# A second pair of tiles for the matrices of the triangular solve in a hybrid RWKV-7 diffusion backbone

## The chip, the cores and the metric

The kernel runs on one core of a Trainium2 chip. The metric is the device time of one execution in microseconds (us), the median of several runs. Engines are named as the profile names them: PE is the TensorE's matmul, PEld its weight load, DVE the VectorE, ACT the ScalarE, POOL the GpSimd, SP the SyncE, whose queue issues the DMA transfers here.

## What is computed

The reference is a backbone of two layers on 1024 latent tokens and 256 context tokens, 1024 wide. A layer makes a combined projection, gives its columns to four mixers (a bidirectional RWKV-7 scan, a pooling, a Fourier and a convolution mixer), concatenates, projects back, and ends in a SwiGLU feed-forward. The change concerns the RWKV-7 scan, a recurrence on a 64 x 64 state for each of four heads and two directions:

```python
def step(S, inp):
    w_t, kk_t, a_t, k_t, v_t = inp[:5]
    sa = jnp.einsum('bhvk,bhk->bhv', S, -kk_t)
    S = (S * w_t[:, :, None, :] + sa[..., None] * (kk_t * a_t)[:, :, None, :]
         + v_t[..., None] * k_t[:, :, None, :])
    y = jnp.einsum('bhvk,bhk->bhv', S, inp[5]) if with_out else None
    return S, y
...
for l in range(DEPTH):
    ...
    y_rwkv_x, y_rwkv_c = _rwkv_mixer(ux[..., :RWKV_COLS], uc[..., :RWKV_COLS], not last, ...)
    h = h + gt1 * _mix_and_project(ux, y_rwkv_x, *other)
    h = h + gt2 * _swiglu(_modulate(h, norm2_g[l], sh2, sc2), ffn_w_in[l], ffn_w_out[l])
```

## The kernel before

The scan is cut into stages: per layer two of the context (c0, c1) and eight of the latent tokens (x0 to x7), each 128 tokens of each direction and all heads. Inside a stage the recurrence is written in chunks of 64 tokens, for which a triangular system has to be solved. `rwkv2` (line 800) goes through the stages with generators that it steps in turn: for the stage at hand it runs `chain` (the states), and at the same time `front_b` and `finish` for its neighbours, `inner` of the stage two ahead and `prep` of the stage three ahead. Between the steps it takes pieces of other work as fill for PE, mostly `outp` (line 1648), the output projection of an earlier unit.

- `prep` (line 896) makes the decays and the scaled keys: tanh on ACT, an affine step on GpSimd (line 921), a running sum on the VectorE (line 926), exponentials on ACT, products on the VectorE and GpSimd (lines 942 to 971).
- `inner` (line 973) makes the matrices and solves. PE forms the Gram products in PSUM; the VectorE masks them (line 991, four instructions); SP stores the parts of interest to DRAM, eight transfers into `Ad` (line 995); SP loads them back in the shape that the solve wants, two transfers of 256 KB into `As` for a = 0 and 1 (line 1001). GpSimd then sets the diagonals to one (line 1029). The 4 x 4 diagonal blocks (lines 1031 to 1035) are solved on the VectorE for a = 0 and on GpSimd for a = 1. Eight steps follow on the VectorE (lines 1043 to 1052); the first four read `As` of a = 0, the last four that of a = 1. The result is stored to `Td` (line 1056) and read back in four transfers (line 1062).
- `front_b` (line 1069) and `chain` (line 1133) use the solved block.

Tiles come from `rg(R, name, depth)` (line 855): a ring of so many tiles under a name, handed out in turn. A ring of depth 1 gives the same tile each time, and the next stage's writer waits until the last reader of this stage is done. Every tile of a ring is a buffer of the pool `t2`, which has 73 of 128 x 512 floats; a ring holds its tiles to the end of the layer's scan. `outp` takes its readings of `ymix` (line 1657) and of the residual (line 1676) from the same pool; each reading of `ymix` is split in two (line 325, on GpSimd during the scan).

The order of instructions on an engine isn't the order of the code. A scheduler takes what is ready by its own estimate, by priorities; the solve (`ahead(SPRI)`) has a priority 1000 ahead of its place, and `pin` keeps some instructions in the order of the program. SP takes the DMA issues one after another, and an issue that waits holds up all behind it.

Of the kernel before, what the change touches and what calls it, by code (L numbers as in the profile page):

```python
# [92 lines left out]
class _Kernel:  # L93
# [879 lines left out]
    def inner(s, R, F):  # L973
# [21 lines left out]
                    nc.sync.dma_start(Ad[b, d, :, h].rearrange("u j i -> j u i"), W[r0:r0 + 32, :, 32 * b:32 * b + 32])  # L995
            yield

        As = [s.rg(R, f"As{a}", 1) for a in range(2)]
        Adf = Ad.rearrange("b d u h j i -> (b d u h) (j i)")
        for a in range(2):  # L1000
            nc.sync.dma_start(As[a], Adf[:, a * 512:(a + 1) * 512].unsqueeze(0).broadcast_to([4, 32, 512]))
# [890 lines left out]
```

## Time and profile before

| | |
|---|---|
| median of 3 runs | 3343.46 us (3340.38 to 3346.46) |
| the profiled execution | 3351.38 us, of which the span is 3349.6 us |
| mean granted clock of PE | 0.911 of full speed |
| PE, PEld busy | 90%, 72% of the span |
| DVE, ACT, POOL busy | 63%, 38%, 41% |
| DMA moved | 415.48 MB, 124 GB/s over the span |
| scan of the first layer | about 489 to 836 us of the span |
| scan of the second layer | about 2168 to 2549 us |

The profile is of one execution, and its times are counted from the start of its span. A chain is the work that ended last, followed back from the end; its shares are of the stretch asked for. A wait is idle time of an engine together with what ended it.

### The profile page before, as it was taken

What the parts mean: (1) busy time and instruction counts of PE and PEld (TensorE: products, weight loads), DVE (VectorE), ACT (ScalarE), POOL (GpSimd) and SP (SyncE); (2) the same over time, 40 slices, a digit from 0 to 9 for tenths busy, and PEclk for the clock granted to TensorE, in tenths of its full rate; (3) what the DMA queues carried; (4) which work ended last, traced back from release to release, by engine and by line L of the source; (5) the groups of instructions that cost most, each with busy time, mean ns of one, the idle gap of its engine ahead of it and who ended that gap; (6) DMA issues with size and microseconds to landing.
All of it is one profiled execution on the core that took longest, in us unless ns stands there. A gap on an engine that the chain in (4) does not pass through costs nothing.

```text
span 3349.6 us, 52386 instructions
## 1 busy us (share of the span) xinstructions
PE 3000.7 (90%) x18888; PEld 2410.5 (72%) x18888; DVE 2109.8 (63%) x3498; ACT 1257.5 (38%) x2575; POOL 1385.8 (41%) x1484
## 2 busy tenths in 40 slices
PE   6989997877889999999999978988877799999998
PEld 3657765766678888888888766756665588888787
DVE  6679666666374988644545598666665755554535
ACT  4446433443363222223212455333443433333212
POOL 2366224563168554435310064245550454545400
PEclk8989887787899999999999988987787799999999
DMA  7422344465455444337412212345553322224312
GB/s 265 165 92 97 102 117 136 124 174 156 144 190 164 149 132 151 125 98 233 139 35 78 87 53 90 117 134 139 156 159 88 128 92 79 82 89 164 123 39 78
DMA packets 375818, 415.48 MB, mean 124 GB/s; under 512 B 115587, under 2 KB 214916, under 8 KB 375558
## 3 DMA queue, kind: packets, MB, share of 16 engines
q1 hardware_dynamic: 375558, 412.13, 39.4%
q8 instruction: 149, 2.44, 0.3%
q14 instruction: 111, 0.91, 0.1%
HBM read 306.49 MB, written 100.27 MB: 121 GB/s over the span
## 4 chain that ended last, share of the span: by engine, by line
PE 55%; DVE 14%; DMA 9%; issue 3%; SPq 1%; ACT 1%; POOL 1%; DVEq 0%; POOLq 0%; ACTq 0%
PE pc L153 17%; PE ps L153 17%; PE pb L153 14%; PE pf L153 8%; DMA t<-Ad 3%; DVE c L532 2%; DMA Td<-t 1%; DVE t L1050 1%; DVE t L947 1%; DVE t L1043 1%; DVE f L325 1%; DVE t L956 1%; DVE t L1469 1%; DMA t<-ho 1%; DVE t L1493 1%
## 5 line engine op out<-in xcount | busy, mean ns | idle before, releaser
L153 PE MATMUL pc<-t,f 128*128 128x512 f32 (+1 forms) x3108 | 754.4, 392 | 41.3 <-ACT t L427 16.0
L153 PEld LDWEIGHTS pc<-t,f 128*128 128x128 f32 x3108 | 581.6, 195 | 182.9 <-ACT t L427 20.5
L153 PE MATMUL ps<-t,f 128*128 128x512 f32 (+1 forms) x2094 | 517.0, 393 | 18.4 <-ACT t L324 7.7
L153 PE MATMUL pb<-t,f 128*128 128x512 f32 (+1 forms) x2094 | 470.5, 370 | 8.4 <-ACT t L1468 4.9
L153 PEld LDWEIGHTS ps<-t,f 128*128 128x128 f32 x2094 | 390.8, 190 | 99.8 <-ACT t L324 8.2
L153 PEld LDWEIGHTS pb<-t,f 128*128 128x128 f32 x2094 | 370.4, 190 | 78.8 <-ACT t L1468 6.0
L1515 ACT CAST f<-c 128x512 fp32r<-128x512 f32 x316 | 196.0, 621 | 536.7 <-PE ps L153 132.0
L1517 POOL TENSOR_TENSOR f<-c,f 128x512 fp32r<-128x512 f32 x135 | 186.5, 1381 | 426.2 <-ACT f L1515 411.7
L153 PE MATMUL pf<-t,f 128*128 128x512 f32 (+2 forms) x1500 | 314.2, 364 | 14.2 <-DVE t L1044 4.0
L324 ACT CAST f<-m 128x512 fp32r<-128x512 f32 (+1 forms) x236 | 134.7, 576 | 436.3 <-PE pb L153 226.4
L153 PEld LDWEIGHTS pf<-t,f 128*128 128x128 f32 (+1 forms) x1500 | 249.5, 198 | 61.4 <-ACT f L324 4.4
L530 POOL TENSOR_TENSOR c<-c,cp 128x352 f32<-128x352 f32 (+2 forms) x168 | 183.3, 1092 | 145.9 <-ACT c L523 71.3
L1517 DVE TENSOR_TENSOR f<-c,f 128x512 fp32r<-128x512 f32 x181 | 158.6, 878 | 134.8 <-ACT f L1515 134.4
L153 PE MATMUL pf<-c,f 128*128 128x512 f32 (+1 forms) x704 | 200.5, 416 | 30.0 <-DVE t L1684 20.3
L325 POOL TENSOR_TENSOR t<-c,t 128x512 fp32r<-128x512 f32 (+1 forms) x110 | 135.1, 1266 | 173.8 <-PE ps L153 99.5
L153 PE MATMUL ps<-t,t 64*128 64x128 f32 (+2 forms) x1032 | 159.9, 341 | 38.9 <-DVE t L956 23.4
L532 DVE SCALAR_TENSOR_TENSOR c<-c,dv,c 128x352 f32<-128x352 f32 (+2 forms) x238 | 190.5, 829 | 2.0
L153 PEld LDWEIGHTS ps<-t,t 64*128 64x128 f32 (+1 forms) x1032 | 133.6, 231 | 60.4 <-issue 20.4
L153 PEld LDWEIGHTS pc<-t,t 128*64 128x64 f32 (+2 forms) x2484 | 124.6, 161 | 71.8 <-issue 28.6
L153 PE MATMUL pc<-t,t 128*64 128x64 f32 (+3 forms) x2484 | 156.2, 258 | 20.9 <-DMA t<-t 11.8
L153 PEld LDWEIGHTS pf<-c,f 128*128 128x128 f32 x704 | 131.5, 214 | 60.1 <-issue 19.1
L261 DVE SCALAR_TENSOR_TENSOR cp<-m,sc,cp 128x512 f32<-128x512 f32 x140 | 137.5, 1003 | 43.0 <-DMA m<-in_wmod 42.3
(256 smaller groups left out, 4731.3 us busy)
## 6 DMA issues: line engine op xcount, KB each, us to landing
c<-in_ffin SPq DMA_DIRECT2D x176, 256.0 KB
m<-in_wmod SPq DMA_DIRECT2D x116, 256.0 KB
t<-rw SPq DMA_DIRECT2D x232, 128.0 KB
hid<-t SPq DMA_DIRECT2D x88, 256.0 KB
c<-hid SPq DMA_DIRECT2D x88, 256.0 KB
m<-in_ffout SPq DMA_DIRECT2D x80, 256.0 KB
t<-in_wmod SPq DMA_DIRECT2D x76, 256.0 KB
m<-in_win SPq DMA_DIRECT2D x64, 256.0 KB
```

Source lines behind the costliest of these rows:

```text
L153: s.nc.tensor.matmul(o, l, r, start=start, stop=stop)
L261: nc.vector.scalar_tensor_tensor(acc[t], w, sc, acc[t], ALU.mult, ALU.add)
L324: r = s.nc.scalar.copy(hi, src)
L325: (eng or s.lo_eng).tensor_tensor(lo, src, hi.bitcast(F32), ALU.subtract)
L530: nc.gpsimd.tensor_tensor(g, g, t_, ALU.add)
L532: nc.vector.scalar_tensor_tensor(a, w[:, j:j + m], tap(j), a, ALU.mult, ALU.add)
L947: nc.vector.scalar_tensor_tensor(KRv[:, :, p, 0, 1:64], k2[:, :, p, 1:64], -2.0, P2[:, :, p, 0:63], ALU.mult, ALU.mult)
L956: nc.vector.tensor_tensor(BKv[rows, :, :, 1 - h, :], cv(kd)[rows], cv(iP)[rows], ALU.mult)
L1043: nc.vector.tensor_tensor(tv, at(x, o, [0, m], [1, 4], [32, 4]), at(T_, r0, [32, m], [0, 4], [1, 4]), ALU.mult)
L1050: nc.vector.tensor_tensor(tv, at(x, o + 4, [0, m], [1, n], [32, 4]), at(T_, r0, [32, m], [0, n], [1, 4]), ALU.mult)
L1515: nc.scalar.copy(hi, x)
L1517: (nc.gpsimd if s.nw % 7 in LOP else nc.vector).tensor_tensor(lo, x, hi.bitcast(F32), ALU.subtract)
```

## The change

`inner` takes its two `As` tiles from rings of depth 2 where they had depth 1. The stages then use two pairs of tiles in turn, and two more buffers of `t2` stay held through each scan. Nothing else in the code differs.

```diff
@@ -995,7 +995,7 @@
                     nc.sync.dma_start(Ad[b, d, :, h].rearrange("u j i -> j u i"), W[r0:r0 + 32, :, 32 * b:32 * b + 32])
             yield
 
-        As = [s.rg(R, f"As{a}", 1) for a in range(2)]
+        As = [s.rg(R, f"As{a}", 2) for a in range(2)]
         Adf = Ad.rearrange("b d u h j i -> (b d u h) (j i)")
         for a in range(2):
             nc.sync.dma_start(As[a], Adf[:, a * 512:(a + 1) * 512].unsqueeze(0).broadcast_to([4, 32, 512]))
```

Each engine has the same instructions as before; within the two scans their order is another. Three places follow. In the rows `Ad`, `Td`, `t`, `m`, `ho`, `hd` stand for the stored matrices, the solved block, tiles of `t2`, weights, the projection's output and the residual; line 302 loads weights, 876 slices of the scan's inputs.

SP in the second layer, around the loads of stage x2, before:

```order
L995 DMA Ad_21190<-t_3735_19993 32x4x32 x2
L995 DMA Ad_21190<-t_3737_19995 32x4x32 x2
L1685 DMA ho_17778<-t_3936_21254 128x512
L302 DMA m_3997_21795<-in_wout 128x512
L1001 DMA t_3662_19537<-Ad_21190 128x1x512
L302 DMA m_4000_21801<-in_wout 128x256
L1001 DMA t_3663_19538<-Ad_21190 128x1x512
L1056 DMA Td_21274<-t_3775_20164 4x256x32
L1676 DMA t_3966_21486<-hd_17788 128x512
L1676 DMA t_3987_21686<-hd_17789 128x512
L1676 DMA t_4003_21807<-hd_17790 128x512
L1062 DMA t_3759_20082<-Td_21274 32x8x32 x4
```

and after:

```order
L995 DMA Ad_21194<-t_3736_19994 32x4x32 x2
L995 DMA Ad_21194<-t_3738_19996 32x4x32 x2
L1056 DMA Td_21278<-t_3779_20168 4x256x32
L302 DMA m_3988_21684<-in_wout 128x256
L876 DMA t_3681_19634<-rw_17820 128x2x128 x2
L1062 DMA t_3761_20084<-Td_21278 32x8x32 x3
L995 DMA Ad_21194<-t_3737_19995 32x4x32 x2
L995 DMA Ad_21194<-t_3739_19997 32x4x32 x2
L1062 DMA t_3761_20084<-Td_21278 32x8x32
L302 DMA m_4001_21799<-in_wout 128x512
L1001 DMA t_3664_19539<-Ad_21194 128x1x512
L1001 DMA t_3665_19540<-Ad_21194 128x1x512
```

The store of the solved block of x1 and three of its four loads have moved ahead of the second four Ad stores and the two loads of x2's matrices.

SP in the first layer, around the loads of stage x7, before:

```order
L995 DMA Ad_7559<-t_701_3188 32x4x32 x2
L995 DMA Ad_7559<-t_703_3190 32x4x32 x2
L1056 DMA Td_7641<-t_749_3454 4x256x32
L1207 DMA t_934_4578<-yb_6665 128x512
L1001 DMA t_721_3288<-Ad_7559 128x1x512
L1001 DMA t_722_3289<-Ad_7559 128x1x512
L1062 DMA t_980_4871<-Td_7641 32x8x32 x4
```

and after:

```order
L1056 DMA Td_7643<-t_749_3454 4x256x32
L995 DMA Ad_7561<-t_701_3188 32x4x32 x2
L876 DMA t_744_3427<-rw_897 128x2x128
L995 DMA Ad_7561<-t_703_3190 32x4x32 x2
L1685 DMA ho_860<-t_1303_7590 128x512
L302 DMA m_1390_8213<-in_wout 128x256
L1062 DMA t_982_4873<-Td_7643 32x8x32 x4
L1001 DMA t_836_4000<-Ad_7561 128x1x512
L1001 DMA t_837_4001<-Ad_7561 128x1x512
```

The loads of the solved block of x6 (line 1062) have changed places with the loads of x7's matrices, and the Td store stands ahead of the last four Ad stores.

GpSimd in the second layer, where the matrices of x1 have landed (`c`, `cp` and `t` in line 325 are the split readings of the output projection), before:

```order
L1029 MEMSET t_3663_19538 128x16
L1031 TENSOR_TENSOR g_20966<-t_3663_19538 128x4x2
L325 TENSOR_TENSOR c_3869_20744<-t_3867_20741,c_3868_20743 128x512
L921 TENSOR_SCALAR t_3609_19247<-t_3609_19247 128x512
L921 TENSOR_SCALAR t_3610_19248<-t_3610_19248 128x512
L325 TENSOR_TENSOR cp_20748<-t_3870_20745,c_3871_20747 128x512
```

and after:

```order
L325 TENSOR_TENSOR c_3873_20748<-t_3871_20745,c_3872_20747 128x512
L1029 MEMSET t_3763_20104 128x16
L1031 TENSOR_TENSOR g_20970<-t_3763_20104 128x4x2
L325 TENSOR_TENSOR cp_20752<-t_3874_20749,c_3875_20751 128x512
L325 TENSOR_TENSOR cp_20756<-t_3877_20753,c_3878_20755 128x512
L1032 TENSOR_TENSOR t_3763_20104<-t_3763_20104,g_20970 128x4
L921 TENSOR_SCALAR t_3611_19249<-t_3611_19249 128x512
```

The two splits into `cp` have moved ahead of line 921, and the split into `c` ahead of the memset.

## Rows read from the trace of the kernel before

**Rows 1.** The page's chain that ended last, shares of the span by line.

```profile
PE pc L153 17%; PE ps L153 17%; PE pb L153 14%; PE pf L153 8%; DMA t<-Ad 3%; DVE c L532 2%; DMA Td<-t 1%; DVE t L1050 1%; DVE t L947 1%; DVE t L1043 1%; DVE f L325 1%; DVE t L956 1%; DVE t L1469 1%; DMA t<-ho 1%; DVE t L1493 1%
```

**Rows 2.** Both scans: length; busy PE, PEld, DVE, ACT, POOL (instructions); clock, DMA share, GB/s.

```profile
489.00:835.80 346.80, 274.38 (x2963) 215.88 (x2962) 218.22 (x511) 141.49 (x381) 168.52 (x284) 0.78 0.52 145
2168.10:2548.70 380.60, 306.37 (x2964) 228.21 (x2966) 249.25 (x577) 150.37 (x398) 181.15 (x314) 0.79 0.51 140
```

**Rows 3.** The chain inside the first and the second scan, shares by line.

```profile
by line: DMA t<-Ad 14.7%; PE pf L153 12.4%; PE pc L153 8.7%; PE ps L153 8.0%; PE pb L153 5.4%; issue 4.1%; DMA Td<-t 2.7%; DVE t L1050 2.6%; DVE t L1052 2.0%; DVE t L926 2.0%; DVE t L1043 1.9%; DVE t L947 1.9%; DMA Ad<-t 1.7%; DVE g L1051 1
...
by line: DMA t<-Ad 12.5%; DMA Td<-t 9.2%; PE pf L153 7.0%; PE ps L153 7.0%; issue 6.7%; DVE t L1050 4.4%; DVE t L956 3.9%; DVE t L1043 3.8%; DVE t L947 3.5%; DVE g L1051 2.9%; DVE t L950 2.9%; PE pc L153 2.7%; DMA t<-rw 2.3%; DVE t L926 2.3
```

**Rows 4.** VectorE waits, first then second scan: total us, times, longest.

```profile
DVE g L1031 <- DMA t<-Ad: 52.3, 6, 11.2
...
DVE g L1031 <- DMA t<-Ad: 53.3, 8, 11.1
```

**Rows 5.** Waits of SP's queue at line 1001, whole span.

```profile
SPq L1001 <- DMA Ad<-t: 5.3, 8, 1.8
SPq L1001 <- DVE t L1044: 2.1, 2, 1.5
```

**Rows 6.** Pieces of the chain, 583 to 720 us: start, length, what.

```profile
628.76 8.47 DMA t<-Ad
...
659.36 2.86 PE pf L153 x12
...
665.30 0.69 DVE t L991
...
669.99 10.09 DMA t<-Ad
```

**Rows 7.** Timeline of SP, then of GpSimd, first layer's x2: start, length.

```profile
581.84 0.56 SPq L1001 DMA_DIRECT2D t<-Ad  x1
...
585.10 0.56 SPq L1001 DMA_DIRECT2D t<-Ad  x1
...
592.45 0.13 POOL L1029 MEMSET t<- 128x16 f32 x1 [3.85 <-DVE t L1043]
```

**Rows 8.** Timeline of SP, second layer's x2.

```profile
2310.28 0.57 SPq L1001 DMA_DIRECT2D t<-Ad  x1
...
2311.67 0.56 SPq L1001 DMA_DIRECT2D t<-Ad  x1
2312.28 0.54 SPq L1056 DMA_DIRECT2D Td<-t  x1
2312.87 8.65 SPq L1676 DMA_DIRECT2D t<-hd  x3
2322.58 1.80 SPq L1062 DMA_DIRECT2D t<-Td  x4
```

**Rows 9.** Timeline of GpSimd at the same place; idle time before it in brackets.

```profile
2319.71 0.14 POOL L1029 MEMSET t<- 128x16 f32 x1 [3.07 <-DMA t<-Ad]
```

**Rows 10.** Timeline of SP, first layer's x7.

```profile
808.75 0.60 SPq L1056 DMA_DIRECT2D Td<-t  x1
...
811.83 1.12 SPq L1001 DMA_DIRECT2D t<-Ad  x2
813.56 1.79 SPq L1062 DMA_DIRECT2D t<-Td  x4
```

**Rows 11.** Timeline of SP, second layer's x6.

```profile
2481.27 1.91 SPq L1062 DMA_DIRECT2D t<-Td  x4
2483.35 1.13 SPq L1001 DMA_DIRECT2D t<-Ad  x2
```

**Rows 12.** Timeline of GpSimd, second layer's x1.

```profile
2280.54 1.29 POOL L325 TENSOR_TENSOR c<-t,c 128x512 fp32r<-128x512 f32 x1
2281.80 1.21 POOL L921 TENSOR_SCALAR t<-t 128x512 f32<-128x512 f32 x2
```

**Rows 13.** GpSimd's waits, 450 to 840 us, at a split for a load.

```profile
POOL f L325 <- DMA t<-rw: 6.7, 1, 6.7
```

## The prediction

> **What bounds the kernel now.** I read the profile from the outside in. The page's chain first: over the whole span the work that ended last is PE's, four groups of matmuls with 17, 17, 14 and 8%, and the two DMA groups that stand highest behind them are the load of the solve's matrices (`t<-Ad`, line 1001, 3%) and the store of its result (`Td<-t`, 1%) [rows 1]. The change can act only where these loads are made, so the windows of the two scans come next: 346.8 us in the first layer and 380.6 us in the second, with PE busy for 274.4 and 306.4 us and a granted clock of 0.78 and 0.79 [rows 2]. About a fifth of PE's time is idle there. Third, the chain inside these windows: the loads at line 1001 are 14.7% of the first and 12.5% of the second, where the store of the solved block adds 9.2% [rows 3]. That is the place to look, and it agrees with the waits: in the first scan the VectorE stood 52.3 us at line 1031 (the first instruction on the matrices) until the load had landed, 53.3 us in the second [rows 4].
>
> The question that decides is why the load lands when it does. It can only be issued when the Ad stores are done, when its tile is free, and when SP reaches it. The SP queue's waits give the answer for the tile: at line 1001 SP waited 2.1 us in two places for the VectorE to let go of a tile, and 5.3 us in eight places for the Ad stores [rows 5]. So the tile is nearly always free when it is wanted. The chain shows the turn of a loop that is closed without it [rows 6]: the load issued at 628.76 takes 8.47 us; when it has landed, GpSimd, which had stood at its memset (line 1029), goes on to the decay's step at line 921 that lies behind it in its queue; the VectorE's preparation, PE's Gram products and at last the mask at line 991 (665.30) follow; the Ad stores, and the next load at 669.99, which takes 10.09 us. One turn is 41.2 us, and the solve that holds the tile isn't in it. The diff frees the tile; it doesn't shorten the turn.
>
> **The waits that it removes.** In the order before, only four of the 40 loads carry a wait on the VectorE for the tile, each the second load (a = 1) of its stage; after, none does. What they cost is read at two of them. At 581.84 the first load goes out, at 585.10 the second, and it has landed when GpSimd starts at 592.45: 7.35 us behind its own issue [rows 7]. In the second layer the pair goes at 2310.28 and 2311.67 and has landed by 2319.71: 8.04 us [rows 8, 9]. Two second loads that didn't wait took 8.47 and 10.09 us from their issue [rows 6]. A load that was held back therefore lands sooner after its issue, by 0.4 to 2.7 us, since the one ahead of it is already further on. Back to back the two issues are about 0.6 us apart (2312.28 less 2311.67 is such a step [rows 8]), so the first wait put the issue back by 2.6 us and won back 1.1 to 2.7 us: it cost at most 1.5 us. Four such places cost at most 6.0 us, at least nothing. I take **-1**.
>
> **What the order of work does.** Every engine has the same instructions as before, but with the tiles free the scheduler puts those of the two scans in another order. The solve's instructions (which have priority) move ahead of others on the VectorE, and with them the store of the solved block (line 1056) on SP. This is where the change acts.
>
> - *Second layer, x2, SP.* Before: eight Ad stores, the two loads at 2310.28 and 2311.67, the Td store of the solve before (2312.28), and the four loads of that solved block at 2322.58, behind 8.65 us of readings of the residual [rows 8]. After: four Ad stores, Td, three loads of the solved block, and only then the other four Ad stores and the loads of line 1001. SP takes its entries in turn, so the matrices now stand behind the landing of Td. Elsewhere that landing let the loads go 4.81 us after the store's issue (808.75 to 813.56 [rows 10]). With Td where it was, 2312.28 + 4.8 + 1.4 (three loads at 0.45) + 2.0 (four Ad stores, at about the 0.5 of any issue here) + 0.8 (a load and a weight's issue) is 2321.3: 11.0 us later than 2310.28. On the other side the solved block is read at 2317.1 and not at 2322.58, 5.5 us earlier, and that is on the path too, since the landing of Td is 9.2% of this scan's chain [rows 3]. Bounds -5.5 and +11.0; I take the net of the two, **+5**.
> - *First layer, x7, SP.* Before, the matrices go at 811.83 and the solved block at 813.56 [rows 10]. After, they change places, so the matrices leave at 813.56 + 1.79 = 815.35. Bounds 0 and +3.5; **+2**, as the second half of the Ad stores comes later on SP as well and may hide the rest.
> - *Second layer, x6, SP.* The opposite: before, four loads of the solved block (2481.27, 1.91 us) stand ahead of the matrices at 2483.35 [rows 11]; after, behind them. Bounds -2.1 and 0; **-1.5**.
> - *Second layer, x1, GpSimd.* Line 921, which began at 2281.80 behind one 1.29 us split [rows 12], now has two splits behind the landing of its load. 2 x 1.29 - 1.29 = **+1.3**; bounds 0 and +2.6, the second if the split that has moved ahead of the landing had hidden in the wait all the same. Queued behind it are the scan at line 926 and the whole preparation of the next stage, that is, the loop.
> - *First layer, x5 and x6.* The preparation of x6 moves ahead of the solve of x5, and PE issues the work of x6 earlier: by its transposes 15 matmuls of output projection fewer have gone ahead. Twelve such took 2.86 us [rows 6], so 15 take 3.6 us. Bounds -3.6 and 0; **-2**. The fill that didn't run is still to be done: by x7 it is 18 matmuls, 4.3 us. They run in PE's idle time (a fifth of the window), or behind the scan; bounds 0 and +4.3, **+1**, near the idle end. In the second layer PE is level again at x7.
> - *Two more tiles of 73 are held through the scan*, so four readings for the second unit of the output projection come in ones and twos and not in a row. The splits that use them lie 8 us and more behind; cost **0** while that holds (rival E has its price).
>
> **The sum** for the profiled execution: -1 + 5 + 2 - 1.5 + 1.3 - 2 + 1 = +4.8 on 3351.4 us, 3356.2. That execution lies 7.9 us over the median of 3343.46, and I carry the difference over as it is: 3343.5 + 4.8 = **3348.3 us**. What a measurement of this kernel can tell from no change is about 0.2%, 6.7 us either way, 3336.8 to 3350.2; the forecast lies inside it, near its upper end.
>
> **The rivals.**
>
> - *C: the loads leave the loop.* If the load were held by its tile, a second pair would let it be issued a stage ahead, and the two idle stretches at line 1031, 52.3 + 53.3 = 105.6 us [rows 4], would go: 3343.5 - 105.6 = 3237.9 us. For it speaks that the gap repeats in every stage; against it that SP waits 2.1 us in all for the tile [rows 5] and that data of a stage can't be loaded before its Ad stores. The Trainium skill has this as a rule ("Perfetto Trace Analysis", Optimization Strategy): consistent bubbles on an engine can mean that there isn't enough SBUF for the next tile to be allocated. The gap is that of the rule, but its releaser here is the transfer and not the tile, so the trace bears it out by those 2.1 us alone. Chance 0.05.
> - *B: a small gain.* In the second layer the path runs through the solved block and not the matrices: x2 gives -5.5, x5 and x6 the whole -3.6, the tile waits -1 and x6 of the second layer -1.5, the rest is hidden: -11.6, 3331.9 us. For it: the 9.2% of the Td landing. Against it: the matrices' 12.5% [rows 3]. Chance 0.13.
> - *D: slower by SP's order.* The matrices behind the landing of Td are the loop itself, and the solved block ahead of them waits anyway. Then x2 costs 11.0, x7 3.5 and line 921 2.6; with -1 - 1.5 - 2 + 1 that is +13.6, 3357.1 us. It decides as soon as the x2 load lands more than some 7 us later than before and nothing else in that turn is later still. For it: the loop has no slack in the chain [rows 6]. Against it: PE had a fifth of idle time to catch up. Chance 0.22.
> - *E: slower by the two lost tiles.* A reading of the output projection waits for a tile, GpSimd stands at its split, and line 921 behind it. The nearest row of GpSimd standing for a reading at a split is one of 6.7 us [rows 13]: 4.8 + 6.7 = +11.5, 3355.0 us. Against it: the cover of 8 us. Chance 0.14.
> - *F: it does nothing.* The tile wasn't wanted and the other orders cancel: 3343.5 us. Chance 0.06, and within 0.2%.
>
> **How the numbers follow.** The forecast has 0.40, so with F 0.46 lie within 0.2%; B and C make 0.18 for faster, D and E 0.36 for slower. The range leaves out C, about half of B and the far part of D: 3333 to 3361 us. The forecast's own range is its sum with one term of the first four at an end, 3342 to 3355.
>
> **What would show it.** Right: no SP wait for the VectorE at line 1001, yet 45 to 55 us at line 1031 in each scan; in the second layer's x2 the matrices leave SP behind the solved block, some 8 us or more after the last mask; the time outside the scans (up to 480 us, 850 to 2160 us, from 2560 us) unchanged. Wrong: if line 1031's idle time falls by more than 15 us in a scan, the tile held more than I read; if a wait for a tile shows at line 1657 with GpSimd idle at line 325, it is E; if the scans change by under 2 us each, the terms above cancel for another reason than the one I give.

## The result and the profile after

The changed kernel took 3365.63 us (median; 3362.98 to 3365.85) beside 3341.92 us (3336.74 to 3346.46) for the kernel before on the same chip: a ratio of 1.007 with a 95% interval of 1.0052 to 1.0087, 23.7 us slower. A repetition gave 1.0074 [1.0055 to 1.0093]. The forecast of 3348.3 us is 17 us short, and the time lies above the range's upper end of 3361.

The page's chain that ended last, after; it answers to [rows 1]:

```profile
PE pc L153 18%; PE ps L153 17%; PE pb L153 14%; PE pf L153 13%; DVE c L532 4%; DMA t<-Ad 3%; DVE f L325 1%; DVE t L1050 1%; DMA Td<-t 1%; DMA t<-ho 1%; DVE t L956 1%; DVE t L1043 1%; DVE t L401 1%; DVE t L947 1%; DMA t<-in_wmod 1%
```

Both scans in the trace of after, cut where those of before were cut (the ends of the last solves before and in the scan); the columns are those of [rows 2]:

```profile
489.90:838.80 348.90, 274.25 (x2964) 212.09 (x2962) 221.41 (x510) 143.16 (x380) 167.45 (x284) 0.79 0.52 144
2171.20:2565.80 394.60, 309.16 (x2972) 232.43 (x2972) 251.37 (x576) 152.61 (x402) 182.47 (x314) 0.78 0.50 135
```

The busy times are those of [rows 2] within 5 us, the clock is the same within 0.01, and the first scan is 2.1 us longer, the second 14.0 us. The rest is idle time, and it isn't at the matrices. The waits after: the VectorE's at line 1031 in the first and the second scan (as [rows 4]), and all that SP waited at line 1001 in the whole span (as [rows 5]):

```profile
DVE g L1031 <- DMA t<-Ad: 44.7, 7, 12.8
...
DVE g L1031 <- DMA t<-Ad: 58.7, 7, 12.3
...
SPq L1001 <- DMA Ad<-t: 6.7, 7, 2.1
```

The 2.1 us of SP's waits for the tile are gone, as the diff says, and the idle time at line 1031 is 44.7 + 58.7 = 103.4 us where it was 105.6. The tile didn't hold the loads.

**Where the time went.** Length of the first scan (end of c1's solve to end of x7's), of the second (c0's to x7's), and of what lies around them, us, read from the solve's lines:

| trace (its own time) | to c1 | scan 1 | between | scan 2 | behind |
|---|---|---|---|---|---|
| before (3351.4) | 489.1 | 346.7 | 1332.3 | 380.6 | 800.8 |
| before, again (3350.7) | 495.5 | 344.9 | 1332.0 | 384.7 | 791.8 |
| before_2 (3356.9) | 489.4 | 348.3 | 1337.5 | 379.7 | 800.2 |
| before_3 (3334.0) | 486.6 | 338.5 | 1333.0 | 381.0 | 793.2 |
| after (3365.6) | 489.9 | 348.9 | 1332.4 | 394.6 | 798.0 |
| after_again (3363.4) | 491.6 | 347.8 | 1337.1 | 397.0 | 788.1 |

Scan 2 is 14 us longer (means 395.8 and 381.5). For scan 1 these six traces give about 4, with one of before as long as after's. But seven of the traces in this document have the VectorE's and GpSimd's order of before throughout the first scan (the four of before, l1only, bpin_x2 and second_from_x2 below), and seven that of after (after, after_again, l0only, fixx2, x2inverted, swapx2 and sp_free_x2): 337.4 to 348.3 us against 347.1 to 350.1, means 342.8 and 348.6. So the new order costs 5.8 us there, and both scans make 20 of the 23.7 us. In the traces themselves less is seen, because the four executions of before that were traced average 3348 us, 6 us above the median.

In scan 2 two stages carry it. From the start of x1's solve to that of x2's it is 49.3 and 48.9 us after, 40.8 to 41.1 before; x7's solve lasts 24.2 and 25.1 us, before 18.1 to 20.4. No other stage of that scan lies more than some 2 us outside the spread of before.

**The stage x2.** The timeline of SP after (start, length, line; as [rows 8] of before):

```profile
2308.80 2.38 SPq L995 DMA_DIRECT2D Ad<-t  x4
2311.26 0.57 SPq L1056 DMA_DIRECT2D Td<-t  x1
2311.93 2.21 SPq L302 DMA_DIRECT2D m<-in_wout  x1
2314.23 1.22 SPq L876 DMA_DIRECT2D t<-rw  x2
2316.08 1.29 SPq L1062 DMA_DIRECT2D t<-Td  x3
2317.47 2.65 SPq L995 DMA_DIRECT2D Ad<-t  x4
...
2321.31 1.16 SPq L1001 DMA_DIRECT2D t<-Ad  x2
```

and the chain of after there (start, length, what):

```profile
2310.99 0.28 DVE t L991
2311.26 4.75 DMA Td<-t
2316.08 0.31 SPq L1062
...
2319.69 1.54 DMA Ad<-t
2321.31 0.56 SPq L1001
2321.92 10.33 DMA t<-Ad
```

The last mask is done at 2312.26, 33.1 us behind the start of x1's solve (2279.13). Before, the row of the last mask was

```profile
2307.36 0.68 DVE L991 TENSOR_TENSOR t<-ps,cv 128x512 f32<-128x512 f32 x1
```

which ends 32.4 us behind the start of x1's solve (2275.65), and in the three other traces of that kernel it is 32.8 to 33.1 us. Up to there nothing clear is lost. Then SP stands: the last four Ad stores, whose data is there, go out at 2317.47, behind the landing of Td, and the matrices at 2321.31, 42.2 us behind x1's solve and not 34.6 (2310.28 [rows 8] less 2275.65).

**The stage x7.** The VectorE at the start of x7's solve, after (idle time before an instruction and what ended it in brackets):

```profile
2542.72 0.18 DVE L1043 TENSOR_TENSOR t<-t,t 128x16 f32<-128x16 f32 x1
2550.75 0.69 DVE L1231 TENSOR_TENSOR t<-t,pb 128x512 f32<-128x512 f32 x1 [7.86 <-PE pb L153]
2551.36 0.16 DVE L1044 TENSOR_REDUCE t<-t 128x4 f32<-128x16 f32 x1
```

and before:

```profile
2530.54 0.18 DVE L1043 TENSOR_TENSOR t<-t,t 128x16 f32<-128x16 f32 x1
2530.76 0.17 DVE L1044 TENSOR_REDUCE t<-t 128x4 f32<-128x16 f32 x1
2532.09 0.69 DVE L1231 TENSOR_TENSOR t<-t,pb 128x512 f32<-128x512 f32 x1 [1.16 <-PE pb L153]
```

After, the solve's second instruction (line 1044) is queued behind line 1231, which finishes x6 and waits for PE. PE's inputs hang on GpSimd, which has its four-by-four blocks for x7 ahead of x6's gate (line 1158). The chain of after has it in this order:

```profile
2536.23 7.94 DMA t<-Ad
...
2545.57 0.22 POOL t L1035
2545.78 0.57 POOL gg L1158
...
2547.08 1.63 PE pc L153 x4
2548.71 2.02 PE pb L153 x8
2550.75 0.70 DVE t L1231
```

So x7's solve on the VectorE waits 7.9 us for work of x6 that itself waited for the second load of x7's matrices.

**The stage x0 of the first layer.** Here the matrices stand behind the four loads of the solved block in both orders, so the hold-up met at x2 can be read without a change of place. Counted from the start of c1's solve, the Td store leaves SP 29.1 to 29.8 us behind it in the seven traces of before's order and 31.7 to 32.6 in those of after's; the matrices leave at 37.9 to 38.6 and at 40.5 to 41.6, and x0's solve begins at 44.0 to 45.4 and at 47.3 to 48.1. The Td store is later because c1's solve ends later on the VectorE (28.5 to 29.3 us behind its start, then 29.8 to 30.5) and because on SP a weight load that waits for PE (1.3 us in after's trace, 0.8 in after_again's) now stands among the Ad stores ahead of it. Some 3 us are lost there.

### The profile page after: what moved, and what is told of

Read it like the earlier page. It is cut to its first block, busy times and chain, and to the rows that moved or that the text cites. A ratio compares the mean times of both kernels' runs of the same rounds, so it can differ in the third digit from the quotient of the medians.

```text
span 3363.8 us, 52373 instructions
## 1 busy us (share of the span) xinstructions
PE 2998.8 (89%) x18888; PEld 2406.5 (72%) x18888; DVE 2111.0 (63%) x3498; ACT 1260.1 (37%) x2575; POOL 1385.6 (41%) x1484
## 4 chain that ended last, share of the span: by engine, by line
PE 62%; DVE 17%; DMA 10%; issue 4%; POOL 2%; ACT 2%; SPq 2%; DVEq 0%; POOLq 0%; ACTq 0%
PE pc L153 18%; PE ps L153 17%; PE pb L153 14%; PE pf L153 13%; DVE c L532 4%; DMA t<-Ad 3%; DVE f L325 1%; DVE t L1050 1%; DMA Td<-t 1%; DMA t<-ho 1%; DVE t L956 1%; DVE t L1043 1%; DVE t L401 1%; DVE t L947 1%; DMA t<-in_wmod 1%
## 5 line engine op out<-in xcount | busy, mean ns | idle before, releaser
L153 PE MATMUL pf<-c,f 128*128 128x512 f32 (+1 forms) x704 | 199.9, 413 | 28.5 <-DVE t L1684 20.4
L153 PEld LDWEIGHTS pc<-t,t 128*64 128x64 f32 (+2 forms) x2484 | 117.3, 151 | 69.0 <-issue 34.2
L153 PE MATMUL pc<-t,t 128*64 128x64 f32 (+3 forms) x2484 | 148.0, 248 | 18.2 <-DMA t<-t 12.2
```

The lines of the kernel that those rows point to most:

```text
L153: s.nc.tensor.matmul(o, l, r, start=start, stop=stop)
```

## The experiments

Every kernel here does the whole computation. "Increment of x2" is the time from the start of x1's solve to that of x2's in the second scan. Traces are of one execution each.

**The kernel before once more, and the change in one layer.**

```diff
-        As = [s.rg(R, f"As{a}", 2) for a in range(2)]
+        As = [s.rg(R, f"As{a}", 2 if R.l == 0 else 1) for a in range(2)]     # l0only
+        As = [s.rg(R, f"As{a}", 1 if R.l == 0 else 2) for a in range(2)]     # l1only
```

> The kernel before, unchanged, for a second trace of it. The first traced execution had a span of 3349.6 us, some 8 us over the median. Expected by every theory: a span of 3335 to 3350 us; the interest is in which stage the two executions differ, and that is the noise against which single stages may be read. If solve ends of the second scan differ by 10 us between two executions of one order, then no loss of after in that scan can be put down to the order.

> Depth 2 for the solve's matrices in the first layer alone, depth 1 in the second. The first scan's SP order is that of after word for word; in the second layer's x2 the matrices leave ahead of the store of the solved block, as in before. Theory Q (the loss comes from SP's order at the second layer's x2, where the matrices stand behind the landing of the solved block): +3 us against before, what after's first scan lost, so within 0.2%. Theory S (two tiles fewer cost in each scan alike): about half of after's loss, +10 to +12. Theory N (any other order than before's is worse, whatever it changes): +10 to +25.

> Depth 2 in the second layer alone. The first scan's order is that of before. In the second layer the waits for the tile are gone as in after, but at x2 and x3 the matrices now leave ahead of the loads of the solved block; from x4 on SP's order is that of after. Theory Q: the 8 us of x2 are not lost, its first solve instruction begins within 3 us of before's 2316.5 us (shifted by what the first scan gives); what after lost from x5 on (4 us) may stay, so +0 to +6. Theory S: the second scan's whole loss, +11 to +14. Theory N: +10 to +25.

The untouched kernel took 3350.69 us in the execution traced, and 3331.88 to 3357.85 us in the 29 runs of the series (median 3344.03). Its second scan, 384.7 us, is 4 us from that of the first trace, against the 14 of the change. l0only: 3353.27 us, 1.0031 [1.0014 to 1.0047], +9.2. l1only: 3341.76 us, 0.9994 [0.998 to 1.0008]. In l1only the second scan has the second pair of tiles and is 382.6 us long, with an increment of x2 of 43.6. Its x7's solve lasts 25.9 us, as long as after's, but x3's increment is 39.1 us (before 44.3 to 44.8): a late x7 alone doesn't make the scan longer. So neither the tiles held there nor the depth as such make it longer; the parts sum to +7 and the whole costs +24. Two kernels with the same code for the second layer have other orders in it, because the scheduler arrives there with another past.

**The suspected queue alone.** In the kernel before, x2's two loads of matrices (line 1001) are kept behind the four loads of x1's solved block (line 1062); both lines get the pin (line 1062 for x1's block), one of them is shown, shortened.

```diff
-            nc.sync.dma_start(As[a], Adf[:, a * 512:(a + 1) * 512]...)
+            (s.pin if (R.l == 1 and F.seg == "x" and F.i == 2) else (lambda q: q))(nc.sync.dma_start(As[a], ...))
```

> The kernel before (depth 1), with one thing forced: in the second layer the loads of x2's matrices stay behind the loads of x1's solved block on SP, and with them behind the landing of its store. No tile is added. Up to there the order is before's. Theory Q: the first solve instruction of x2 comes 8 to 12 us later than before and the scan ends 8 to 12 us later: +8 to +12. Theory S: 0, as no tile is taken. Theory N: +10 to +25, but with the loss in other stages as well.

SP there:

```profile
2302.48 0.60 SPq L1056 DMA_DIRECT2D Td<-t  x1
...
2307.35 1.80 SPq L1062 DMA_DIRECT2D t<-Td  x4
2309.19 1.12 SPq L1001 DMA_DIRECT2D t<-Ad  x2
```

The increment of x2 became 49.8 us, the same as after, with tiles and depth as before; scan 2 was 392.5 us. The order on SP is enough to make x2 late. What that costs isn't settled by this run. The pin changed later places too: x3's increment is 32.8 us, which gives back 12, x4's is 46.6 and x7's solve lasts 25.0. The time is 3348.08 us, 1.0017 [0.9998 to 1.0036], +4, where +8 to +12 were expected: the interval reaches from nothing to +12 us.

**The change without its x2, and with x2 alone out.** fixx2 keeps depth 1 in the second layer up to x1, x2inverted keeps it there for x0 to x3; after_again is the change itself.

```diff
-        As = [s.rg(R, f"As{a}", 2) for a in range(2)]
+        As = [s.rg(R, f"As{a}", 2 if R.l == 0 or (F.seg == "x" and F.i > 1) else 1) for a in range(2)]      # fixx2
+        As = [s.rg(R, f"As{a}", 1 if R.l == 1 and F.seg == "x" and F.i < 4 else 2) for a in range(2)]      # x2inverted
```

> The kernel after, unchanged, timed in more rounds and traced once more, beside the variants of this series. Against before: +15 to +25 if the first four times were typical; +8 to +15 if the 4 times of before had been low ones (before runs from 3332 to 3358 us on the chip of the first series). Theory Q (SP's order at the second layer's x2): the first solve instruction of x2 comes again some 8 us later, measured from that of x1, than in before (there 40.8 us after x1's), and the second scan takes some 8 to 14 us longer than before's 380.6 and 384.8 us (from the end of c0's solve to the end of x7's).

> The kernel after, with one ring taken back for a while: in the second layer the stages c0, c1, x0 and x1 use one pair of tiles, from x2 on two in turn; the first layer as in after. At x2 the matrices now leave ahead of the store of the solved block, as in before; x3 and x4 are ordered as in after, x6 has the matrices behind the solved block. Theory Q: the 8 us of x2 come back: some 8 to 12 us faster than after, +3 to +12 against before. Theory S (two tiles fewer): slower than before by all of after's loss, as both pairs are held in the first scan and from x2 on. Theory M (the loss of the second scan is from x5, where the masks stand behind the solve on the VectorE): no faster than after, as x5 is ordered like it.

> The other half: depth 2 as in after, but in the second layer x0 to x3 use one pair; x2 and x3 are ordered as in after (the matrices of x2 behind the landing of the solved block), while x4 to x6 are ordered as in before. Theory Q: the loss of x2 stays, 8 to 12 us in the second scan; against before +12 to +20, within 4 us of after. Theory M: the loss is gone, +3 or so against before, by the first scan. Theory S: as after.

after_again: 3366.13 us, +24.8 against before in its series, increment 48.9, as expected.

fixx2: 3359.42 us, 1.0051 [1.0032 to 1.0069]; increment 40.0, x7's solve 19.0, scan 2 385.1: the second scan has nearly the length of before again, and 6.7 us of 24.8 are back. That is less than the 11 us by which its second scan is shorter, and 18 us remain, of which its scans show 9 (735.2 us in all; before 726.1 on average). So taking x2 and x7 out is worth 6.7 us in time in this kernel, and not the 13 that their stages show. x2inverted: 3362.59 us, 1.0067 [1.0044 to 1.0091], increment 49.3: it has depth 1 at x2 and still has the late x2, since its order on SP there is that of after, with other tiles' names. The depth at x2 doesn't decide whether it is late; the order does.

**More of the suspected queue.** In pin_all all Ad stores and both kinds of loads are pinned as written, so that in every stage the matrices stand behind the solved block of the stage before; in lagged the loads of line 1062 are written two steps later and both kinds of loads are pinned, so that the matrices go first at all latent stages but the first layer's x7 and, in part, the second layer's x3.

```diff
+        for _ in range(2):          # lagged, ahead of the loads at line 1062
+            yield
```

> The kernel after, with the suspected cost made general: on SP the loads of each stage's matrices are kept behind the loads of the solved block that precede them in the program, so that they wait for the landing of its store in nearly every stage. Theory Q: a landing takes about 5 us, 10 at worst; in 10 of the 16 latent stages the matrices leave behind the solved block that did not in before, so +40 to +80 against before. If the loop had slack, and the loss of after came from tiles or from elsewhere, under +15 more than after.

> The kernel after, with the loads of each solved block put two steps later in the program and held on SP behind the loads of the next stage's matrices. In all latent stages but three (first layer's x7, second layer's x3 in part) the matrices then leave ahead of the solved block. Theory Q, carried to all stages: as fast as before or faster, 3330 to 3345 us. Rival: the solved block's loads are as urgent as the matrices', and every stage loses there what it gains here: within 5 us of after.

Neither did what the theory of SP's order said. pin_all, expected far slower than after, took 3359.89 us, 1.0071 [1.0044 to 1.0099], with a scan 2 of 383.6 and a scan 1 of 357.1. lagged, expected at 3330 to 3345 us if the theory held everywhere, took 3365.96 us, 1.0075 [1.006 to 1.009]; its x2 came at 52.7. That is what the rival in its expectation says, within 5 us of after. In pin_all's second scan the matrices stand behind the solved block at every stage and x2's increment is 48.8, and the scan is no longer than before's. As a general rule, "matrices behind the solved block is slow" is false.

**The queue put right in the changed kernel.** swapx2: for the second layer's x2 alone, the loads of x1's solved block are written one step later, and stores and loads are pinned. sp_free_x2 also pins the slices of the inputs (line 876) and the weight loads (line 302) of that turn.

> The kernel after, with seven issues of SP put in another order at one place: in the second layer the second four Ad stores and the two loads of x2's matrices go ahead of the four loads of x1's solved block, so that they no longer stand behind its landing. PE and ACT move one or two rows, VectorE and GpSimd six at the same place, all else is after's order. In both traces of after the last Ad store of x2 was issued 148.5 to 148.9 us after the end of c0's solve and x2's solve began at 155.9 to 157.3; in five traces without that order 140.3 to 142.8 and 146.7 to 150.8. Theory Q: the solve of x2 begins 5 to 6 us earlier, at 150 to 152 (SP stood 5.2 us for the landing), the rest of the 8 us having come from masks that were late before it; the scan is 5 to 12 us shorter than 394.6 and 397.0, and the time 5 to 12 us under after's 3366. If the order at x2 were only a sign of another loss, the scan would stay within 2 us of after's.

> The kernel after, where SP keeps the program's order at the second layer's x2 among Ad stores, matrices, solved block and weights: all eight Ad stores go out with one other entry between them, then two weights, the store of x1's solved block, the matrices, and behind them the loads of that block. The later stages of that scan get other orders too (x3's eight Ad stores in a row, x4 and x6 with the matrices ahead of the solved block); the first scan is after's. If SP's queue held x2 back: its solve 40 to 43 us behind x1's (49 in after), the scan some 8 us shorter than after's 395 to 397, the time 3354 to 3360 us (after 3366, before 3341). If something ahead of the masks held it: 47 us or more at x2.

swapx2: 3361.24 us, 1.007 [1.0054 to 1.0085], increment 48.8. Its timeline of SP:

```profile
2310.90 2.65 SPq L995 DMA_DIRECT2D Ad<-t  x4
2313.64 0.57 SPq L1056 DMA_DIRECT2D Td<-t  x1
2314.30 2.23 SPq L302 DMA_DIRECT2D m<-in_wout  x1
2316.62 1.23 SPq L876 DMA_DIRECT2D t<-rw  x2
2317.94 1.02 SPq L302 DMA_DIRECT2D m<-in_wout  x2
2319.06 1.80 SPq L995 DMA_DIRECT2D Ad<-t  x4
2323.65 1.15 SPq L1001 DMA_DIRECT2D t<-Ad  x2
2324.85 1.94 SPq L1065 DMA_DIRECT2D t<-Td  x4
```

The loads of the solved block now stand last, and the Ad stores still leave at 2319.06, 4.6 us behind the last mask (2314.48). Ahead of them stand the inputs' slices and the weight loads, and in the chain it is ScalarE's line 324 (2317.05, 0.53 us) that releases these. So the edit didn't move the matrices, which leave 42.6 us behind x1's solve (after 42.2), and scan 2 is 395.1 us, as after; the run says nothing on what an earlier issue is worth. It does show something else: the solved block was read 6.8 us later in the stage's own time than in after's trace, and the next two increments, 44.8 and 37.7, are those of after (44.3 and 37.9).

sp_free_x2: 3361.67 us, 1.0073 [1.0056 to 1.009], and the increment of x2 is 54.1 us. But its matrices were early. GpSimd there (line 1030 is its line 1029 of the others):

```profile
2323.14 0.13 POOL L1030 MEMSET t<- 128x16 f32 x1 [2.43 <-DMA t<-Ad]
2326.43 0.13 POOL L1030 MEMSET t<- 128x16 f32 x1 [3.16 <-DMA t<-Ad]
...
2327.80 0.63 POOL L922 TENSOR_SCALAR t<-t 128x512 f32<-128x512 f32 x1
...
2328.56 1.54 POOL L922 TENSOR_SCALAR t<-t 128x512 f32<-128x512 f32 x1
```

and the VectorE (each line one higher):

```profile
2313.58 0.29 DVE L1045 TENSOR_REDUCE t<-t 128x32 f32<-128x128 f32 x1
2328.46 1.23 DVE L927 TENSOR_TENSOR_SCAN t<-t,t 128x512 f32<-128x512 f32 x1 [14.59 <-POOL t L922]
...
2335.11 0.16 DVE L1032 TENSOR_TENSOR g<-t 128x8 f32<-128x8 f32 x1
```

The first matrix had landed by 2323.14, 42.2 us behind the start of x1's solve (2280.97; after: by 2328.48, 49.3). Yet the solve begins at 2335.11: with the new issue times the scheduler put the next stage's preparation ahead of it on the VectorE, and that stood 14.59 us for GpSimd's line 922, itself queued behind both landings. The queue was put right, the gain arrived at the VectorE's door, and another queue took it. Neither of the two expected outcomes came: the wait lay behind the masks.

**The tiles' number and which tiles.** a1only gives the second tile to a = 1 alone, where before had its four waits; b72 is the kernel before with 72 tiles in the pool, nothing freed; second_from_x2 has depth 2 in the second layer from x2 on.

```diff
-        As = [s.rg(R, f"As{a}", 2) for a in range(2)]
+        As = [s.rg(R, f"As{a}", 1 + a) for a in range(2)]      # a1only
+        As = [s.rg(R, f"As{a}", 2 if R.l == 1 and F.seg == "x" and F.i > 1 else 1) for a in range(2)]      # second_from_x2
-T2 = 73
+T2 = 72      # b72, in the kernel before
```

> A second tile for a = 1 alone (depth 1 for a = 0), in both layers: all four waits for a tile are gone, one buffer more is held and not two. The order of the first scan's x0 and x1 is that of after; at x2 of the second layer the matrices leave behind the loads of the solved block. Theory Q with the first scan's order: x1's solve in the first layer begins 67 to 69 us after the end of c1's (60 to 66 in the traces of before's order), x2's in the second layer 154 to 158 us after c0's; the time is +10 to +22 against before. Theory S (the buffers): half of after's loss, +10 to +12, with x2 of the second layer at 147 to 151.

> The kernel before with 72 buffers in the pool and not 73, and one pair of tiles: a buffer fewer, nothing freed. SP's order is before's up to the first layer's x4, other orders come behind; at x2 of the second layer the matrices leave ahead of the solved block's loads or between them and its store. Theory Q: x2 of the second layer at 147 to 152 us, the first scan 337 to 347 us, the time within 8 us of before. Theory S: +10 to +12. Theory N (any other order than before's is worse): +10 to +25.

> Depth 1 everywhere but in the second layer from x2 on, where two pairs are used in turn. The order is that of before up to the second layer's x3 and that of after from x4 on, x7's place among it. If the two losses of the second scan add up: x2 at 40 to 42 us behind x1, x7's solve 24 to 26 us long, the scan 386 to 390 us, +3 to +8 against before. If one alone is covered by what else bounds the scan: 381 to 387 us and within 4 us of before. If the loss comes with the tiles held and not with the order: +10 or more.

a1only: 3364.33 us, 1.0073 [1.0058 to 1.0088]; most of its loss lies in scan 1 (356.3), and scan 2 has 387.2. b72: 3364.35 us, 1.008 [1.0065 to 1.0095]; x2 is in time (41.7), and x5 and x6 are late (56.0 and 45.8 us; before 48.8 and 40.7). One buffer fewer and nothing else costs as much as the change, at another place. second_from_x2: 3346.16 us, 1.0021 [1.0003 to 1.0038], +8.5; scans of 339.7 and 384.3. Its x2 is in time (40.7), and its x7's solve lasts 19.2 us as before, not the 24 to 26 expected of it.

**Without GpSimd in the solve.** The memset of line 1029 (for both matrices) and lines 1031 to 1035 of a = 1 go to the VectorE, in the changed kernel and in the one before, so that a landing holds up no queue of GpSimd.

```diff
-            e, x = (nc.vector, nc.gpsimd)[a], As[a][:, :]
+            e, x = nc.vector, As[a][:, :]
...
-            s.pin(nc.gpsimd.memset(at(x, 16 * a, [33, 16]), 1.0))
+            s.pin(nc.vector.memset(at(x, 16 * a, [33, 16]), 1.0))
```

> The kernel after, with the memset of the diagonals (line 1029, both halves) and the small solve of a = 1 (lines 1031 to 1035) on the VectorE. GpSimd no longer stands for the matrices' load; its idle time at line 1029 (some 170 us over the span in before) goes. If that queue closes the loop: line 921 begins before the load lands, each latent stage gets 2 to 4 us shorter, 30 to 60 us faster than after in all. If not: 7 more short instructions of about 0.2 us on the VectorE in each of 20 stages, up to +28 us, mostly beside waits, so within 10 us of after.

> The same edit in the kernel before, one pair of tiles. If GpSimd's queue closes the loop: 30 to 60 us faster than before. And whether the second pair is worth something once that queue is free: dve_after would then be faster than this one; if the tile never held anything, within the spread of the orders, some 10 to 20 us either way.

dve_after: 3356.23 us, 1.0057 [1.0038 to 1.0076]; dve_before: 3360.71 us, 1.0072 [1.0052 to 1.0092]. The large gain expected isn't there; the kernel before loses 23 us by it. With that edit in both, the second pair isn't slower: 4.5 us in its favour, with intervals that overlap.

**Where the loss lies, over all kernels.**

> The kernel before, unchanged, for another trace. Theory S: what the changed order costs lies in the two scans, wherever in them. Over the traces of 16 kernels the sum of both scans' lengths (from c1's solve to x7's solve in the first layer, c0's to x7's in the second) runs with the timed difference, 1.05 us per us; by that line an execution of the kernel before near its median of 3342 us has 722 to 726 us of scans, against 743.5 and 744.8 in the two traces of the changed kernel, and one near 3351 us (as both traced so far) has 727 to 730. Theory T: the difference lies outside the scans as well: then an execution near the median has scans of 727 or more and some other stretch 5 us shorter than 1332 (between the scans) or 790 (behind them).

> As the run before it: a further trace of the unchanged kernel. S: 722 to 726 us of scans if the execution lies at 3338 to 3345 us, 727 to 730 if at 3350. T: 727 or more in either case.

The two executions took 3356.88 and 3334.01 us, with scans of 728.0 and 719.5 us in all (table above). The second has 8 to 10 us less of scan than the other three, most of it in scan 1, and lies below the median; between and behind the scans it is like the others. That goes with S, though neither execution lies near the median, where S and T were to be told apart. The first, 15 us over the median, has no longer scans than those at 3351, but 5 us more between them; behind them it has 800.2 us, as the first trace (800.8), where the two others have 791.8 and 793.2. So part of the spread of the kernel before itself lies elsewhere, as T has it. Sum of both scans in the trace, against the timed difference from the kernel before in the same series:

| kernel | scans, us | timed difference, us |
|---|---|---|
| before (four traces) | 719.5 to 729.6 | 0 |
| second_from_x2 | 724.0 | +8.5 |
| l1only | 726.7 | -2.3 |
| bpin_x2 | 729.9 | +4.0 |
| l0only | 732.2 | +9.2 |
| fixx2 | 735.2 | +18.1 |
| dve_after | 737.7 | +18.5 |
| pin_all | 740.7 | +18.6 |
| dve_before | 741.0 | +23.0 |
| b72 | 741.2 | +24.2 |
| after, after_again | 743.5, 744.8 | +23.7, +24.8 |
| a1only | 743.5 | +24.1 |
| swapx2 | 744.4 | +21.0 |
| sp_free_x2 | 744.5 | +24.0 |
| x2inverted | 746.0 | +21.3 |
| lagged | 747.8 | +25.8 |

Over these sixteen changed traces the correlation is 0.91 and the slope 1.05 us of time for one of scan; single kernels lie up to 7 us off that line (second_from_x2 above it, l1only below). Most of the loss is in the scans. Where in the scans is another matter for each kernel: x2 and x7 of the second layer and the start and end of the first scan (after), x5 and x6 (b72), mostly the first layer (a1only, pin_all).

## Why the prediction was wrong, step by step

The forecast is 17 us short. Two steps failed. At x2 a gain was netted against the loss: +5 was taken, +7 to +8.5 measured. And the sum put at nothing the stages for which no term was written, x7 of the second layer (+5 us) and x0, x1 and the last solve of the first scan (some +8), though the new order reaches them too. The second is the larger.

- **What bounds the kernel: right.** The loads didn't leave the loop: 103.4 us of idle time at line 1031 for 105.6 (44.7 and 58.7 us, where 45 to 55 were named for each scan). Rival C falls by these rows: more SBUF was given, and the bubbles stayed. The Trainium skill ("Perfetto Trace Analysis", Optimization Strategy) states that consistent bubbles on the engine that should be saturated can mean that there isn't enough SBUF or PSUM for the next tile. The trace doesn't agree for these bubbles, which are on the VectorE: 103.4 of 105.6 us stayed.
- **The waits for the tile, -1: too small to be seen.** They are gone. One of the two rows that it was worked out from is a bound only: GpSimd's start at 592.45 was released by the VectorE [rows 7], so the load may have landed before.
- **Second layer's x2, +5: mis-sized, the first step that failed.** The issue of the matrices behind the landing of Td came as worked out (2316.08 for the loads of Td, 4.8 us behind its store, then four Ad stores, then 2321.31). Against the start of x1's solve it was 7.6 us late, within the bound of 11.0. What failed is the netting: I took 5.5 us off because the solved block is read earlier. It was read 10.0 us earlier in the stage's own time (37.0 us behind x1's solve, before 46.9), and x2's solve began 8.5 us later all the same; the next two stages gave back 1.8 us at most (44.3 and 37.9 us for 44.8 and 39.2). Swapx2, which read it 6.8 us later than after at no loss, shows the same from the other side. Of the 9.2% of `Td<-t` in the chain of [rows 3], one stretch of 10.2 us lies there. With the landing at 4.75 us the chain of after runs through the matrices instead; a share of the chain isn't the gain from shortening it. Rival D, which left the netting out, had the direction and came nearer to this term (11.0), but its 3357.1 us are still 8.5 short; it had only 0.22.
- **x7 of the second layer, no term: +5 us.** I followed the loads on SP and put the end of the scan at nothing. The solve's line 1044 behind line 1231 is a wait that the order shows and that I didn't look for. That its 5 us are a loss of as much time is read from the trace and not tried by itself; in l1only another stage gave them back.
- **First layer: x7 +2 measured 0, x5 and x6 -2 about right, but no term for the start and the end, the second step that failed.** The two loads changed places as said (the matrices at 812.59 behind the solved block at 810.58), and x7's increment is 44.9 for 45.2. x5 and x6 take 45.0 and 50.1 for 46.3 and 51.8. x0 loses some 3 us (48.1 and 47.3; before 44.2 to 45.3), x1 1 to 6 (51.1 and 51.4; before 45.1 to 50.0), and x7's solve 2 (20.0 and 19.7; before 17.5 to 18.7). The terms of this scan add up to +1, the seven traces of either order give +5.8. What makes x0 late is read above from fourteen traces; for x1 and the last solve the cause is open.
- **Line 921 at x1, +1.3: right in itself.** Its row after:

```profile
2284.05 2.50 POOL L325 TENSOR_TENSOR cp<-t,c 128x512 fp32r<-128x512 f32 x2
...
2286.66 1.43 POOL L921 TENSOR_SCALAR t<-t 128x512 f32<-128x512 f32 x2
```

  It is 7.5 us behind x1's solve, before 6.1. The scan of line 926 behind it came 3.6 us later, since the solve's steps now stand ahead of it on the VectorE, and still the last mask was at most 0.7 us late: there is slack in the preparation.
- **Layer two's x6, -1.5: nothing.** The matrices do go first now (2496.37, then 2498.12), and the increments are 42.3 and 41.3 us, before 40.3 to 41.5.
- **The lost tiles, 0: right as far as the tiles go.** The wait of [rows 13] at line 325 is gone from the first scan (one of 7.6 us for a weight load stands at that line now), and l1only holds the two tiles through the second scan and costs nothing. But b72 shows that one tile fewer can cost 24 us by the order it brings. Rival E had the wrong mechanism; the price of a pool's size wasn't in it.
- **The sum.** Terms of single stages were added as if the order elsewhere stayed. In nearly every kernel here something else moved too. x2 and x7 together make about 13 us of scan 2, and the order of the first scan 5.8; some 4 of the 24 aren't found. The forecast's own range also has a slip: with x2's term at its lower bound it goes down to 3338 us, not 3342.
- **The base.** The profiled execution of before, 7.9 us over the median, was carried over as it was. Part of these 8 us lies in a stretch that has nothing to do with the change (below), part in a first scan of 346.7 us, where a faster execution has 338.5.

Open: why taking x2 and x7 out (fixx2) gave back only 6.7 us, and why most of the other orders tried cost 10 to 20 us of scan (l1only, second_from_x2, bpin_x2 and l0only don't). A reading that fits, and isn't shown, is that the old order suits these queues by its estimates or by luck, and that the turn of the loop has several in-order queues of about equal length, so that a disturbance of any of them shows; swapx2 and sp_free_x2 show two such hand-overs (SP to ScalarE's tiles, SP to the VectorE), but not that it is so everywhere.

## What to carry over

Before a ring is made deeper, read what its writer really waited for: 2.1 us of waits for the tile against 105 us of waits for the transfer say that the depth can give little. Where a scheduler orders the work, any change of a pool or a ring is also another order on every in-order queue, and its cost can be ten times the wait removed (here 23.7 us for 2.1); compare, for each stage, what stands between the last input and the next issue on each queue, the compute engines included. At x2 a gain on one branch of a join was worth next to nothing while the other branch was late: bound such a term by its two ends, and don't net them.

## What the runs showed of the hardware

One and the same instruction was stretched fifteen-fold in some executions of the same kernel. In before_2 a split on the VectorE behind the scans (start, length):

```profile
3107.58 11.58 DVE L325 TENSOR_TENSOR f<-m,f 128x512 fp32r<-128x512 f32 x1 [3.22 <-ACT f L324]
```

and in before_3 the same place:

```profile
3092.87 0.77 DVE L325 TENSOR_TENSOR f<-m,f 128x512 fp32r<-128x512 f32 x1 [2.92 <-ACT f L324]
```

GpSimd ran its own splits of line 325 without a gap in both; in before_2

```profile
3103.71 14.90 POOL L325 TENSOR_TENSOR t<-c,t 128x512 fp32r<-128x512 f32 x12
```

Windows of before_2 over that stretch (length; busy PE, PEld, DVE, ACT, POOL; granted clock, DMA share, GB/s):

```profile
3098.00:3107.00 9.00, 9.00 (x41) 7.48 (x40) 2.77 (x4) 5.57 (x10) 9.00 (x8) 1.00 1.05 386
3107.00:3119.00 12.00, 4.97 (x22) 3.77 (x21) 11.42 (x1) 3.67 (x8) 11.61 (x10) 0.84 0.10 31
3119.00:3124.00 5.00, 4.79 (x15) 3.88 (x16) 4.00 (x7) 0.62 (x1) 0.78 (x1) 0.70 0.68 194
```

PE stands for 7 of the 12 us, its granted clock falls from 2.4 GHz (1.00) to a mean of 0.70 in the 5 us behind it, and the time behind the scans is 800.2 us where before_3 has 793.2. Four of the twenty traces have the stretch (before, before_2, after and bpin_x2, 10.9 to 11.6 us), and their time behind the scans is 798.0 to 800.8 us; in the sixteen without it, it is 787.8 to 793.7. In all four the stretched split ends 0.55 us behind the end of GpSimd's row of splits (in before_2 at 3119.16 and 3118.61). That GpSimd's row holds it fits this and isn't shown: in before_3 the same split took 0.77 us beside such a row. Why it is held in some executions and not in others wasn't tried.
